# Gate one-hots of a retrieval layer: 24 narrow tensor_scalar instructions per step exchanged for two wide tensor_tensor instructions

## The chip, the cores and the metric

The kernel runs on one core of one Trainium2 chip. The time is device microseconds of one launch; three launches of the kernel before gave a median of 1547.26 us (1546.43 to 1547.27). Inside the core five engines work from queues of their own, in the order in which the program was written: TensorE (PE, with its weight loads as PEld), VectorE (DVE), ScalarE (ACT), GpSimd (POOL) and SyncE (SP). They wait for each other by semaphores.

## The reference

Two transformer-like blocks over 256 tokens of width 1024. The change lies in the second half of the first block, a retrieval over 128 x 128 single-neuron experts:

```python
s = einsum('thpk,hpnk->thpn', q, sub_keys)          # 8 heads, 2 key halves, 128 keys
sv, si = top_k(s, 16)                               # per half
cand = sv[..., 0, :, None] + sv[..., 1, None, :]    # 256 sums, the best 16 kept
fv, fpos = top_k(cand, 16)
eidx = take_along_axis(si0 * 128 + si1, fpos)       # 16 experts per token and head
g = softmax(fv)
act = gelu(einsum('td,thkd->thk', x, u_tab[eidx]))
y = einsum('thk,thkd->td', g * act, v_tab[eidx])
```

The kernel does not gather. It computes the activation of all 16384 experts for all tokens from the whole table `peer_u`, multiplies by a gate matrix that is zero for experts that were not chosen, and multiplies by the whole table `peer_v`.

## The kernel before, in words

Each of the 128 blocks of `peer_u` (128 experts, a weight tile of 128 x 1024) is one call of `U(b)`: 24 matmuls of 256 columns (L163 to L165, three products of split halves `whi`, `wlo`, `hi`, `lo` over eight pieces), then a GELU on ACT (L793). The halves of a weight tile are made ahead: ACT casts `whi` (L112, five tiles ahead), DVE subtracts `wlo` (L120, four tiles ahead).

The gate matrix is built for one token at a time. For token t there are 128 choices (8 heads x 16), one per partition: a row index, a column index and a gate value. With `o` the one-hot of the second index, and `go` the one-hot of the first index times the gate, the product of `o` and `go` over the partitions is the token's 128 x 128 gate matrix. The gate is kept as two 16-bit halves, so there are two `go` and two matmuls a token (L958). `onehots(og)` makes these tiles for eight tokens (OG = 8): per token one `tensor_scalar` for `o` (L941, compare the constant row 0..127 in `iob` with the index) and two for `go` (L943, compare and multiply), 24 in all. ACT then moves each bank of four tokens from PSUM to `stg`, scaled (L961), and every second step `stg` goes to DRAM as `gd` (L963).

The loop has 32 steps. In program order a step is: the one-hots of the next step, 16 gate matmuls in two groups of eight with an ACT move behind each, then one `U(b)`, which begins with the `whi` and `wlo` of later tiles. The `side` PSUM banks of the gate matmuls and the `main` banks of U are two each. Once the 32 steps are done, seven more U follow, and the loop over `peer_v` starts, which reads the gates back (`gt`). Nothing is scheduled by a planner: each engine's order is that of the code.

Of the kernel before, what the change touches and what calls it, by code (L numbers as in the profile page):

```python
# [13 lines left out]
F32 = mybir.dt.float32  # L14
F32R = mybir.dt.float32r
BF = mybir.dt.bfloat16
F16 = mybir.dt.float16
# [3 lines left out]
OP = mybir.AluOpType  # L21
# [4 lines left out]
T = 256  # L26
# [9 lines left out]
UKEEP = 7  # L36
TG = 16
OG = 8
GI = 8
LOADS = 9  # L40
SPLITS = 4
# [23 lines left out]
class Kx:  # L65
# [696 lines left out]
    def peer(self):  # L762
        nc, tc, a = self.nc, self.tc, self.a
# [4 lines left out]
        drp = ctx.enter_context(tc.tile_pool(name="pdr", bufs=1, space=DRAM))  # L768
        c1 = ExitStack()
        pz = c1.enter_context(tc.tile_pool(name="pz", bufs=1))  # L770
        gp = pz.tile([128, 2, T], F32, name="gp")
        ib = pz.tile([128, 2, T], F32, name="ib")
        acts = {}
        c2 = ExitStack()
        pk = c2.enter_context(tc.tile_pool(name="pk", bufs=1))
# [14 lines left out]
        def U(b):  # L790
            p = self.unit("peer_u", b, h)
            acts[b] = t = actp.tile([128, T], F32, name="act")
            nc.scalar.activation(t, p, AF.Gelu)  # L793

        pre = deque(range(2, NPRE))
        with c2:
# [39 lines left out]
            for hd in range(1, 8):  # L836
# [5 lines left out]
                for i in range(2 if hd > 1 else 0):  # L842
                    p = self.unit("w_query", 2 * hd + i, h)
# [11 lines left out]
            pf_ = c2.enter_context(tc.tile_pool(name="pf", bufs=1))  # L855
# [4 lines left out]
            def finish():  # L860
                g = [pf_.tile([128, 8, 16], F32, name=f"g{tt}") for tt in range(2)]
                pf = [pf_.tile([128, 2, 8, 16], F32, name=f"pf{tt}") for tt in range(2)]
                sxf = [pf_.tile([128, 2, 8, 16], F32, name=f"sxf{tt}") for tt in range(2)]
                for tt in range(2):
                    v = fv[tt]
                    nc.vector.tensor_tensor(g[tt], v, v[:, :, 0:1].to_broadcast([128, 8, 16]), op=OP.subtract)
                    nc.scalar.activation(g[tt], g[tt], AF.Exp)
                for tt in range(2):
                    pi = pft.tile([128, 2, 8, 16], U32, name="pi")
                    nc.vector.tensor_scalar(pi[:, 0], fx[tt], 4, None, op0=OP.logical_shift_right)  # L870
                    nc.vector.tensor_scalar(pi[:, 1], fx[tt], 15, None, op0=OP.bitwise_and)
                    nc.vector.tensor_copy(sxf[tt].rearrange("p s h a -> p h s a"), sx[tt])
                    nc.vector.tensor_copy(pf[tt], pi)
                for tt in range(2):
                    gz = pft.tile([128, 8], F32, name="gz")
                    nc.vector.tensor_reduce(gz, g[tt], axis=AX.X, op=OP.add)
                    nc.vector.reciprocal(gz, gz)
                    nc.vector.tensor_tensor(g[tt], g[tt], gz[:, :, None].to_broadcast([128, 8, 16]), op=OP.mult)
                for _ in range(FW):
                    yield  # L880
                for tt in range(2):
                    p = self.side()
                    for j, src in enumerate((sxf[tt][:, 0], sxf[tt][:, 1], pf[tt][:, 0], pf[tt][:, 1])):
                        nc.tensor.transpose(p[:, j * 128:(j + 1) * 128], src.rearrange("p a b -> p (a b)"),
                                            self.ident)
                    ts = slice(tt * 128, (tt + 1) * 128)
                    p = p.rearrange("p (k s t) -> p k s t", k=2, s=2)
                    nc.scalar.copy(sxT[:, :, ts], p[:, 0])
                    nc.scalar.copy(posT[:, :, ts], p[:, 1])
                p = self.side()  # L890
                for tt in range(2):
                    nc.tensor.transpose(p[:, tt * 128:(tt + 1) * 128], g[tt].rearrange("p a b -> p (a b)"),
                                        self.ident)
                slot = pf_.tile([128, T], F32, name="slot")
                nc.scalar.mul(slot, p[:, :T], GSCALE)
                yield
                acc = self.bank(0)
                last = None
                for a0 in range(0, 16, FA):
                    cur = []  # L900
                    for a in range(a0, a0 + FA):
                        pb = self.side()
                        nc.tensor.matmul(pb, pick[:, a].rearrange("p h w -> p (h w)"),
                                         sxT.rearrange("p s t -> p (s t)"), start=True, stop=True)
                        t = pft.tile([128, 2 * T], BF, name="hit", bufs=2 * FA)
                        nc.vector.scalar_tensor_tensor(t, posT.rearrange("p s t -> p (s t)"), float(a), pb,
                                                       op0=OP.is_equal, op1=OP.mult)
                        cur.append((a, t))
                    yield
                    for a, t in cur:  # L910
                        nc.tensor.matmul(acc, identb, t, start=a == 0, stop=a == 15)
                nc.scalar.copy(ib, acc.rearrange("p (j t) -> p j t", j=2))
                g16 = pf_.tile([128, T], F16, name="g16")
                nc.vector.tensor_copy(g16, slot)
                nc.vector.tensor_copy(gp[:, 0], g16)
                nc.vector.tensor_tensor(gp[:, 1], slot, gp[:, 0], op=OP.subtract)

            self.side_cycle = ("s", "s", "a1", "a2")
            self.tasks.append(finish())
            while self.tasks:  # L920
                self.tick()
                if len(pre) > T // OG + UKEEP:
                    U(pre.popleft())
            while len(pre) > T // OG + UKEEP:
                U(pre.popleft())
            self.side_cycle = ("s",)

        with ExitStack() as c3:
            pg = c3.enter_context(tc.tile_pool(name="pg", bufs=1))
            pgt = c3.enter_context(tc.tile_pool(name="pgt", bufs=2))  # L930
            iob = pg.tile([128, 128], F16, name="iob")
            nc.gpsimd.iota(iob, pattern=[[1, 128]], base=0, channel_multiplier=0,
                           allow_small_or_imprecise_dtypes=True)
            stg = None

            def onehots(og):
                o = pgt.tile([128, OG, 128], F16, name="o")
                go = pgt.tile([128, OG, 2, 128], F16, name="go")
                for i in range(OG):
                    t = slice(og * OG + i, og * OG + i + 1)  # L940
                    nc.vector.tensor_scalar(o[:, i], iob, ib[:, 1, t], None, op0=OP.is_equal)  # L941
                    for j in range(2):
                        nc.vector.tensor_scalar(go[:, i, j], iob, ib[:, 0, t], gp[:, j, t],  # L943
                                                op0=OP.is_equal, op1=OP.mult)
                return o, go

            nxt = onehots(0)
            for og in range(T // OG):
                o2, go = nxt
                if og + 1 < T // OG:  # L950
                    nxt = onehots(og + 1)
                if og % (TG // OG) == 0:
                    stg = pgt.tile([128, 128, TG], F32, name="stg")
                for q in range(OG // 4):
                    p = self.side().rearrange("p (t i) -> p t i", t=4)
                    for i in range(4):
                        for j in range(2):
                            nc.tensor.matmul(p[:, i], o2[:, q * 4 + i], go[:, q * 4 + i, j],  # L958
                                             start=i == 0 and j == 0, stop=j == 1, skip_group_check=True)
                    e0 = (og % (TG // OG)) * OG + q * 4  # L960
                    nc.scalar.mul(stg[:, :, e0:e0 + 4].rearrange("p i t -> p t i"), p, 1.0 / GSCALE)  # L961
                if og % (TG // OG) == TG // OG - 1:
                    nc.scalar.dma_start(gd[:, og * OG // TG], stg)  # L963
                if len(pre) > UKEEP:
                    U(pre.popleft())
# [3 lines left out]
        with ExitStack() as c4:  # L969
# [5 lines left out]
            def gload(i):  # L975
                if i * GI < NB:
                    gts[i] = gt = pv.tile([128, 8 * (T + 2)], F32, name="gt")[:, :8 * T].rearrange(
                        "p (g e) -> p g e", g=T // TG)
                    (nc.gpsimd if i < 2 else nc.scalar).dma_start(gt, gd[:, :, i * GI:(i + 1) * GI].rearrange("p g i t -> p g (i t)"))

            wts = {}

            def w_mult(b):
                if b >= NB:
                    return
                t = acts[b]
                gv = gts[b // GI][:, :, (b % GI) * TG:(b % GI + 1) * TG]
                tv = t.rearrange("p (g t) -> p g t", t=TG)
                nc.vector.tensor_tensor(tv, tv, gv, op=OP.mult)  # L989
                if b % GI == GI - 1:  # L990
                    gload(b // GI + 2)

# [583 lines left out]
```

## Time and profile before

| what | value |
|---|---|
| median of three launches | 1547.26 us |
| the profiled launch, own time | 1546.58 us |
| its span, first to last instruction | 1544.9 us |
| PE / PEld / DVE / ACT / POOL busy, share of the span | 92% / 87% / 78% / 50% / 16% |
| the 32 gate steps, first gate matmul to the last U's first matmul | 382.85 to 570.04 us |
| granted clock in that stretch | 0.94 |

Busy shares are averages over stages; a matmul's recorded duration overlaps the next one's, so that PE reads busy when it is well under its best rate. For PE the start-to-start distance of its instructions is the better measure, and the same holds for DVE and ACT where an instruction's record reaches over the start of the next.

### The profile page before, as it was taken

How to read it: one execution, taken by the hardware profiler on the slowest of the kernel's cores; microseconds unless marked ns; L12 is line 12 of the kernel's file. 1: busy time of each engine (PE TensorE's matmuls, PEld its weight loads, DVE VectorE, ACT ScalarE, POOL GpSimd, SP SyncE). 2: the span in 40 equal slices, each digit the busy share in tenths (PEclk: the TensorE clock that was granted, in tenths of full speed). 3: DMA queues.
4: the chain of work that ended last, by engine and by line, in shares of the span. 5: the costliest groups of instructions: out<-in, count | busy, mean ns of one | idle time of the engine just before them, and what ended most of it. 6: DMA issues, size and time to landing. Idle time of an engine off the chain costs nothing.

```text
span 1544.9 us, 28187 instructions
## 1 busy us (share of the span) xinstructions
PE 1427.4 (92%) x11206; PEld 1351.2 (87%) x11208; DVE 1204.3 (78%) x2723; ACT 765.9 (50%) x1225; POOL 240.9 (16%) x143
## 2 busy tenths in 40 slices
PE   3897888979998999999999999999989989999997
PEld 2777777978777779999999999999989979989997
DVE  7887789997999996777777776666689968775554
ACT  3445554434555555544444454454564485554443
POOL 1443253310000000000000000000057740310000
PEclk8898989989999999999999999999999999999999
DMA  9365543434444458888888887677534434435642
GB/s 377 141 239 181 191 150 136 154 122 162 161 167 186 169 206 308 297 307 312 303 308 286 294 285 233 219 244 241 179 114 163 164 109 164 164 138 190 205 165 81
DMA packets 106068, 317.36 MB, mean 205 GB/s; under 512 B 5584, under 2 KB 34640, under 8 KB 103632
## 3 DMA queue, kind: packets, MB, share of 16 engines
q1 hardware_dynamic: 65696, 250.54, 45.8%
q10 hardware_dynamic: 39408, 61.87, 11.4%
q0 software_dynamic: 832, 3.15, 0.6%
q8 instruction: 88, 1.44, 0.4%
q14 instruction: 44, 0.36, 0.1%
HBM read 297.71 MB, written 17.83 MB: 204 GB/s over the span
## 4 chain that ended last, share of the span: by engine, by line
PE 56%; DVE 34%; ACT 4%; DMA 3%; issue 2%; POOL 1%; DVEq 0%; SPq 0%; ACTq 0%; POOLq 0%
PE a L163 10%; PE a L164 10%; PE a L165 10%; PE m L163 8%; PE m L164 8%; PE m L165 8%; DVE go L943 7%; DVE wlo L120 5%; DVE a L1138 3%; DVE o L941 3%; DVE junk L326 2%; DMA mraw<-in_ada_w 1%; ACT whi L112 1%; DMA raw<-in_ada_w 1%; DVE mdt L294 1%
## 5 line engine op out<-in xcount | busy, mean ns | idle before, releaser
L163 PE MATMUL m<-hi,whi 128*128 128x256 f32 x1816 | 526.5, 290 | 9.2 <-DVE cacc L556 6.0
L165 PE MATMUL m<-hi,wlo 128*128 128x256 f32 x1816 | 516.9, 285 | 9.4 <-DVE wlo L120 9.4
L164 PE MATMUL m<-lo,whi 128*128 128x256 f32 x1816 | 517.0, 285 | 0.0
L112 ACT CAST whi<-raw 128x1024 fp32r<-128x1024 f32 x428 | 444.6, 1046 | 50.1 <-DMA raw<-in_peer_v 19.5
L120 DVE TENSOR_TENSOR wlo<-raw,whi 128x1024 fp32r<-128x1024 f32 x350 | 437.7, 1269 | 30.9 <-ACT whi L112 23.0
L163 PEld LDWEIGHTS m<-hi,whi 128*128 128x128 f32 x1816 | 352.1, 194 | 16.1 <-issue 5.4
L165 PEld LDWEIGHTS m<-hi,wlo 128*128 128x128 f32 x1816 | 351.1, 193 | 10.7 <-DVE wlo L120 10.4
L164 PEld LDWEIGHTS m<-lo,whi 128*128 128x128 f32 x1816 | 351.7, 194 | 0.6
L165 PE MATMUL a<-wh,wlo 128*128 128x256 f32 x1024 | 288.2, 281 | 0.0
L164 PE MATMUL a<-wl,whi 128*128 128x256 f32 x1024 | 288.2, 281 | 0.0
L163 PE MATMUL a<-wh,whi 128*128 128x256 f32 x1024 | 287.9, 281 | 0.0
L120 POOL TENSOR_TENSOR wlo<-raw,whi 128x1024 fp32r<-128x1024 f32 x81 | 202.2, 2510 | 223.0 <-ACT whi L112 196.1
L165 PEld LDWEIGHTS a<-wh,wlo 128*128 128x128 f32 x1024 | 192.9, 188 | 0.0
L164 PEld LDWEIGHTS a<-wl,whi 128*128 128x128 f32 x1024 | 192.7, 188 | 0.0
L163 PEld LDWEIGHTS a<-wh,whi 128*128 128x128 f32 x1024 | 192.7, 188 | 0.0
L1001 DVE TENSOR_TENSOR wl<-act,wh 128x256 fp32r<-128x256 f32 x128 | 54.5, 426 | 140.5 <-PE a L164 125.7
L793 ACT ACTIVATE act<-m 128x256 f32<-128x256 f32 x126 | 48.5, 385 | 197.6 <-PE m L165 197.4
L943 DVE TENSOR_SCALAR go<-iob,ib,gp 128x128 f16<-128x128 f16 x512 | 138.8, 319 | 0.0
L996 ACT CAST wh<-act 128x256 fp32r<-128x256 f32 x128 | 51.9, 406 | 141.7 <-DVE act L989 118.8
L326 DVE SCALAR_TENSOR_TENSOR junk<-mraw,silu 128x1024 bf16<-128x1024 f32 x80 | 104.2, 1303 | 6.3 <-DMA mraw<-in_ada_w 6.0
L220 POOL TENSOR_TENSOR act<-act 128x256 f32<-128x256 f32 x7 | 5.6, 800 | 548.7 <-ACT act L211 548.3
L958 PE MATMUL s<-go,o 128*128 128x128 f16 x512 | 74.1, 219 | 18.3 <-DVE go L943 17.5
(438 smaller groups left out, 1962.0 us busy)
## 6 DMA issues: line engine op xcount, KB each, us to landing
raw<-in_peer_u SPq DMA_DIRECT2D x64, 1024.0 KB, 5.8
raw<-in_peer_v SPq DMA_DIRECT2D x64, 1024.0 KB, 5.3
mraw<-in_w_ada ACTq DMA_DIRECT2D x48, 512.0 KB, 5.8
raw<-in_w_ffn_in SPq DMA_DIRECT2D x22, 1024.0 KB, 5.1
gd<-stg ACTq DMA_DIRECT2D x16, 1024.0 KB, 3.9
gt<-gd ACTq DMA_DIRECT2D x14, 1024.0 KB, 8.7
mraw<-in_ada_w SPq DMA_DIRECT2D x24, 512.0 KB, 3.8
raw<-in_w_ffn_out SPq DMA_DIRECT2D x11, 1024.0 KB, 5.0
```

Source lines behind the costliest of these rows:

```text
L112: self.nc.scalar.copy(t, self.raw[k])
L120: eng.tensor_tensor(t, self.raw.pop(k), h.bitcast(F32), op=OP.subtract)
L163: mm(out, w[0], x[0], start=start, stop=False, **kw)
L164: mm(out, w[0], x[1], start=False, stop=False, **kw)
L165: mm(out, w[1], x[0], start=False, stop=stop, **kw)
L326: self.nc.vector.scalar_tensor_tensor(junk, w, 0.5, self.silu_c[i], op0=OP.mult, op1=OP.mult, accum_out=self.mod[i][:, u:u + 1])
L793: nc.scalar.activation(t, p, AF.Gelu)
L941: nc.vector.tensor_scalar(o[:, i], iob, ib[:, 1, t], None, op0=OP.is_equal)
L943: nc.vector.tensor_scalar(go[:, i, j], iob, ib[:, 0, t], gp[:, j, t], op0=OP.is_equal, op1=OP.mult)
L958: nc.tensor.matmul(p[:, i], o2[:, q * 4 + i], go[:, q * 4 + i, j], start=i == 0 and j == 0, stop=j == 1, skip_group_check=True)
L996: nc.scalar.copy(wts[b], acts[b])
L1001: nc.vector.tensor_tensor(wl, acts.pop(b), wts[b].bitcast(F32), op=OP.subtract)
```

## The change

The indexes and both gate halves of all tokens are kept in one 16-bit tile `ig` instead of two float32 tiles. A new helper `spread(c)` has ACT write the values of 16 tokens out eight times each, side by side, into a tile `rep`. `onehots` then makes its tiles with two wide instructions over 2048 16-bit elements a partition: one `is_equal` gives the one-hots of both indexes, one `mult` multiplies the first of them by both gate halves. Repeated operands have a stride of zero on an outer dimension; the innermost run is eight elements long. The line numbers of the changed kernel are higher, by 2 ahead of this place and by 16 behind it.

```diff
+RC = 16
+RW = 8
...
-        gp = pz.tile([128, 2, T], F32, name="gp")
-        ib = pz.tile([128, 2, T], F32, name="ib")
+        ig = pz.tile([128, 2, T, 2], F16, name="ig")
+        ib, gp = ig[:, 0], ig[:, 1]
...
-                nc.scalar.copy(ib, acc.rearrange("p (j t) -> p j t", j=2))
-                g16 = pf_.tile([128, T], F16, name="g16")
-                nc.vector.tensor_copy(g16, slot)
-                nc.vector.tensor_copy(gp[:, 0], g16)
-                nc.vector.tensor_tensor(gp[:, 1], slot, gp[:, 0], op=OP.subtract)
+                nc.scalar.copy(ib.rearrange("p t j -> p j t"), acc.rearrange("p (j t) -> p j t", j=2))
+                nc.vector.tensor_copy(gp[:, :, 0], slot)
+                nc.vector.tensor_tensor(gp[:, :, 1], slot, gp[:, :, 0], op=OP.subtract)
...
+            rep = {}
+
+            def spread(c):
+                if c < T // RC:
+                    sh = [128, 2, RC * 2, RW]
+                    rep[c] = t = pgt.tile(sh, F16, name="rep")
+                    s = ig[:, :, c * RC:(c + 1) * RC].rearrange("p k t j -> p k (t j)")
+                    nc.scalar.copy(t, s[:, :, :, None].to_broadcast(sh))
+
             def onehots(og):
-                o = pgt.tile([128, OG, 128], F16, name="o")
+                c, r = divmod(og * OG, RC)
+                if r == 0:
+                    spread(c + 1)
+                sh = [128, 2 * OG, 128 // RW, RW]
+                i8, g8 = [rep[c][:, k, 2 * r:2 * (r + OG)][:, :, None, :].to_broadcast(sh) for k in range(2)]
+                o = pgt.tile([128, OG, 2, 128], F16, name="o")
                 go = pgt.tile([128, OG, 2, 128], F16, name="go")
-                for i in range(OG):
-                    t = slice(og * OG + i, og * OG + i + 1)
-                    nc.vector.tensor_scalar(o[:, i], iob, ib[:, 1, t], None, op0=OP.is_equal)
-                    for j in range(2):
-                        nc.vector.tensor_scalar(go[:, i, j], iob, ib[:, 0, t], gp[:, j, t],
-                                                op0=OP.is_equal, op1=OP.mult)
-                return o, go
+                v = lambda x: x.rearrange("p t j (a b) -> p (t j) a b", b=RW)
+                io = iob[:, None, :].to_broadcast([128, 2 * OG, 128]).rearrange("p t (a b) -> p t a b", b=RW)
+                nc.vector.tensor_tensor(v(o), i8, io, op=OP.is_equal)
+                nc.vector.tensor_tensor(go.rearrange("p t j (a b) -> p t j a b", b=RW),
+                                        o[:, :, 0:1].to_broadcast([128, OG, 2, 128]).rearrange("p t j (a b) -> p t j a b", b=RW),
+                                        g8.rearrange("p (t j) a b -> p t j a b", j=2), op=OP.mult)
+                return o[:, :, 1], go
+
+            spread(0)
```

On DVE, the order at the entry to the gate steps and through the first two sets of one-hots, of the kernel before (`wlo` is the subtraction for later U tiles):

```order
L120 TENSOR_TENSOR wlo<-raw,whi 128x1024 x6
L941 TENSOR_SCALAR o<-iob,ib 128x128
L943 TENSOR_SCALAR go<-iob,ib,gp 128x128 x2
...
L941 TENSOR_SCALAR o<-iob,ib 128x128
L943 TENSOR_SCALAR go<-iob,ib,gp 128x128 x2
L120 TENSOR_TENSOR wlo<-raw,whi 128x1024
```

The same place on DVE in the changed kernel:

```order
L122 TENSOR_TENSOR wlo<-raw,whi 128x1024 x6
L955 TENSOR_TENSOR o<-rep,iob 128x2048
L956 TENSOR_TENSOR go<-o,rep 128x2048
L955 TENSOR_TENSOR o<-rep,iob 128x2048
L956 TENSOR_TENSOR go<-o,rep 128x2048
L122 TENSOR_TENSOR wlo<-raw,whi 128x1024
```

The 24 narrow rows of a set have become two wide ones; the rows around them stand where they stood.

On ACT, the first three gate steps of the kernel before, from the GELU of the last U ahead of them:

```order
L793 ACTIVATE act<-m 128x256
L961 ACTIVATE stg<-s 128x4x128 x2
L112 CAST whi<-raw 128x1024
L793 ACTIVATE act<-m 128x256
L961 ACTIVATE stg<-s 128x4x128 x2
L963 DMA gd<-stg 128x2048
L112 CAST whi<-raw 128x1024
L793 ACTIVATE act<-m 128x256
L961 ACTIVATE stg<-s 128x4x128 x2
```

The same place on ACT in the changed kernel:

```order
L795 ACTIVATE act<-m 128x256
L943 COPY rep<-ig 128x512 x2
L977 ACTIVATE stg<-s 128x4x128 x2
L114 CAST whi<-raw 128x1024
L795 ACTIVATE act<-m 128x256
L943 COPY rep<-ig 128x512
L977 ACTIVATE stg<-s 128x4x128 x2
L979 DMA gd<-stg 128x2048
L114 CAST whi<-raw 128x1024
L795 ACTIVATE act<-m 128x256
L977 ACTIVATE stg<-s 128x4x128 x2
```

Two copies to `rep` stand behind the GELU of the U ahead of the first gate step, and one more in every second step, ahead of that step's moves to `stg`. The order on PE is unchanged.

## Rows read from the trace of the kernel before

**Rows 1.** The page: the chain that ended last, shares by line.

```profile
PE a L163 10%; PE a L164 10%; PE a L165 10%; PE m L163 8%; PE m L164 8%; PE m L165 8%; DVE go L943 7%; DVE wlo L120 5%; DVE a L1138 3%; DVE o L941 3%; DVE junk L326 2%; DMA mraw<-in_ada_w 1%; ACT whi L112 1%; DMA raw<-in_ada_w 1%; DVE mdt L294 1%
```

**Rows 2.** Busy time by stretch, inside and behind the gate steps.

```profile
core 0: us, PE busy (x) PEld busy (x) DVE busy (x) ACT busy (x) POOL busy (x), PEclk, DMA share, GB/s
...
480.00:490.00 10.00, 9.29 (x62) 8.05 (x62) 10.00 (x42) 5.49 (x6) 0.00 (x0) 0.83 0.51 185
...
580.00:590.00 10.00, 10.00 (x87) 10.00 (x86) 4.99 (x8) 4.83 (x9) 0.23 (x1) 1.00 1.02 331
```

**Rows 3.** Groups by line, 380 to 620 us: busy, mean ns, idle before, releaser.

```profile
L943 DVE TENSOR_SCALAR go<-iob,ib,gp 128x128 f16<-128x128 f16 x512 | 138.8, 319 | 0.0
...
L958 PE MATMUL s<-go,o 128*128 128x128 f16 x512 | 74.1, 219 | 18.3 <-DVE go L943 17.5
...
L941 DVE TENSOR_SCALAR o<-iob,ib 128x128 f16<-128x128 f16 x256 | 66.2, 259 | 0.0
```

**Rows 4.** DVE in time order: start us, duration us, instruction [idle before <-releaser].

```profile
473.30 0.54 DVE L943 TENSOR_SCALAR go<-iob,ib,gp 128x128 f16<-128x128 f16 x2
473.74 1.23 DVE L120 TENSOR_TENSOR wlo<-raw,whi 128x1024 fp32r<-128x1024 f32 x1
474.88 0.26 DVE L941 TENSOR_SCALAR o<-iob,ib 128x128 f16<-128x128 f16 x1
...
479.75 1.23 DVE L120 TENSOR_TENSOR wlo<-raw,whi 128x1024 fp32r<-128x1024 f32 x1
```

**Rows 5.** PE in time order, the same step.

```profile
471.85 0.43 PE L958 MATMUL s<-go,o 128*128 128x128 f16 x2 [0.17 <-DVE go L943]
...
473.92 0.36 PE L163 MATMUL m<-hi,whi 128*128 128x256 f32 x1
...
476.83 0.85 PE L958 MATMUL s<-go,o 128*128 128x128 f16 x8
```

**Rows 6.** PE, the first ten gate matmuls of the stage.

```profile
382.85 0.73 PE L958 MATMUL s<-go,o 128*128 128x128 f16 x10
```

**Rows 7.** ACT in time order: two moves to `stg` and what is behind them.

```profile
390.03 1.10 ACT L961 ACTIVATE stg<-s 128x512 f32<-128x512 f32 x1 [0.50 <-PE s L958]
...
391.60 1.05 ACT L112 CAST whi<-raw 128x1024 fp32r<-128x1024 f32 x1 [0.47 <-DVE go L943]
...
396.04 1.10 ACT L961 ACTIVATE stg<-s 128x512 f32<-128x512 f32 x1 [1.40 <-PE s L958]
396.92 1.08 ACT L112 CAST whi<-raw 128x1024 fp32r<-128x1024 f32 x1
```

**Rows 8.** ACT in time order, ahead of the gate steps.

```profile
342.98 1.04 ACT L112 CAST whi<-raw 128x1024 fp32r<-128x1024 f32 x1
343.92 0.39 ACT L793 ACTIVATE act<-m 128x256 f32<-128x256 f32 x1
344.19 0.38 ACT L888 CAST sxT<-a 128x256 bf16<-128x256 f32 x1
...
366.09 0.59 ACT L912 COPY ib<-a 128x512 f32<-128x512 f32 x1 [0.49 <-PE a L911]
366.57 1.05 ACT L112 CAST whi<-raw 128x1024 fp32r<-128x1024 f32 x1
...
383.05 0.39 ACT L793 ACTIVATE act<-m 128x256 f32<-128x256 f32 x1 [1.51 <-PE m L165]
```

**Rows 9.** DVE in time order, two of the preparing instructions.

```profile
365.27 0.28 DVE L914 CAST g<-slot 128x256 f16<-128x256 f32 x1
...
365.92 0.43 DVE L916 TENSOR_TENSOR gp<-slot,gp 128x256 f32<-128x256 f32 x1
```

**Rows 10.** PE, the first matmul of the last gate step's U.

```profile
570.04 0.37 PE L163 MATMUL m<-hi,whi 128*128 128x256 f32 x1
```

**Rows 11.** Busy time by stretch, a PE pause ahead of the stage.

```profile
334.00:336.00 2.00, 0.00 (x0) 0.00 (x0) 2.00 (x10) 0.00 (x0) 0.00 (x0) 1.00 0.00 0
336.00:338.00 2.00, 0.00 (x0) 0.00 (x0) 2.00 (x11) 0.00 (x0) 0.00 (x0) 0.59 0.00 0
```

## Prediction

> **What bounds the kernel now.** I read the chain of waits first: nearly all of it is PE, but 7% and 3% of the span are the narrow one-hot instructions L943 and L941 on DVE [rows 1]. So there is a stage in which DVE sets the pace. The table of busy time by stretch says where: inside the gate steps DVE is busy 10.00 of 10 us, PE less, and PE's granted clock falls to 0.83; behind them PE is at 10.00 with clock 1.00 and DVE at half [rows 2]. The groups by line show who waits: PE's gate matmuls stand idle for the releaser DVE L943, while both DVE groups have no idle time ahead of them [rows 3]. Recorded durations overlap, so I work with start-to-start distances.
>
> On DVE one step goes from one `wlo` to the next: 479.75 - 473.74 = 6.01 us. Of this `wlo` takes 474.88 - 473.74 = 1.14, and the 24 narrow instructions 4.87, or 0.203 each [rows 4]. On PE the gate matmuls come two at a time, each pair waiting for its token's one-hots; U itself runs from 473.92 to the next step's first gate matmul at 476.83, 2.91 us [rows 5]. What would the 16 gate matmuls take if nothing held them? The first ten of the stage, whose one-hots were ready, span 0.73 us; one of them lasts 0.219 [rows 3, 6], so they start (0.73 - 0.219) / 9 = 0.057 apart, and 16 take 0.91. With 0.03 for the turn to U, **PE needs 2.91 + 0.91 + 0.03 = 3.85 us a step and DVE makes it wait for 6.01.** That difference is what the change can win; behind the stage PE is full, so time won there is kept to the end.
>
> **The change, part by part.**
>
> *The wide instructions.* No row shows VectorE on two 16-bit tensors. The nearest row by operation is `wlo`, a float32 `tensor_tensor`: 1.23 us for 1024 elements against 0.43 for 256 [rows 4, 9], so 1.04 ns an element, which is 1.07 of its 1.14 us and leaves 0.07 fixed. At that rate 2048 elements take 2.13 + 0.07 = 2.20 us start to start. The nearest rows by element type are the casts to or from 16 bits: 256 elements in 0.28 us where `tensor_tensor` needs 0.43 [rows 9]. Taking the same 0.16 (0.43 less 256 at 1.04 ns) off both, the cast has 0.12 left for what costs 0.27 at one element a cycle, so it does two. At two, 2048 elements take 1.07 + 0.07 = 1.14, the same as `wlo`. The narrow rows don't decide: 128 elements at one a cycle plus 0.07 would be 0.20, which is their mean. I take two a cycle, because both sources and the result are 16-bit and run along consecutive addresses innermost, as in the casts; 2.20 stays as the other end.
>
> [...]
>
> The second wide instruction reads what the first wrote, so it starts behind the first's full duration (1.23) with some 0.05 for the semaphore. **DVE's new step: 1.23 + 0.05 + 1.14 + 1.14 (`wlo`) = 3.56 us**, under PE's 3.85. It stays under as long as the two wide instructions together cost no more than 2.71.
>
> *The copies to `rep` on ACT.* Each has 512 elements, one in two steps. The cheapest comparable row is the 512-element copy `ib`, 366.57 - 366.09 = 0.48 us start to start [rows 8]; the dearest is the strided move to `stg`, also 512, 396.92 - 396.04 = 0.88 [rows 7]. ACT's other work in two steps: GELU 344.19 - 343.92 = 0.27 and `whi` 343.92 - 342.98 = 0.94, twice each [rows 8]; four moves at 0.88; and the issue of the `gd` DMA, which makes one move cost 391.60 - 390.03 = 1.57 and so adds 0.69 [rows 7]. Sum 0.54 + 1.88 + 3.52 + 0.69 = 6.63, with a copy 7.11 to 7.51, against PE's 2 x 3.85 = 7.70. ACT stays just under; a copy above 1.07 us would make it the bound. In the loop each copy is made two steps ahead of its use, so its lateness costs DVE nothing.
>
> *The start.* Here the copies are not ahead. In program order both stand on ACT behind the GELU of the U in front of the gate steps. That GELU starts at 383.05 [rows 8], after PE reached the gate matmuls at 382.85 [rows 6]; before, DVE had made one-hots ahead of that. Now: copy from 383.05 + 0.27 = 383.32, done 0.6 later (the `ib` copy lasted 0.59) at about 383.95; first wide instruction to 385.2, second to 386.5. **PE stands still 3.65 us once**; with the dear copy 4.1. Such a pause can lower PE's clock: in the pause ahead of the stage the granted clock was 1.00 in the first two microseconds without a matmul and 0.59 in the next two [rows 11]. A dip like the one in the stage, 0.83 over 10 us [rows 2], is 3.4 us at half speed and gives away 1.7; I put 2 us, between 0 (none) and 5 (a dip three times as long).
>
> *Preparation.* One cast of 0.28 us goes, and the index copy now writes 16-bit elements two apart, at most 0.4 dearer by the ratio of the two ACT prices above. ACT waits 1.51 us ahead of its GELU there [rows 8], which covers it. Price nothing; 0.4 if the cover were gone.
>
> *Transfers.* The same bytes in shorter time: a DMA share of 0.51 and 185 GB/s become 0.51 x 6.01 / 3.85 = 0.80 and 289 GB/s; behind the stage the queues carry 331 GB/s with PE still at 10.00 [rows 2]. Price nothing.
>
> **The sum.** Before, PE goes from 382.85 [rows 6] to the last step's U at 570.04 [rows 10]: 187.2 us, which is 31 steps and one set of gate matmuls. After: 31 x 3.85 + 0.94 = 120.3, plus 3.65 for the start and 2 for the clock, 125.9. Saved: 61.3 us. The profiled launch took 1546.58 us, so 1485.3; it lies 0.7 under the median, so 1486 on the median's scale.
>
> **The rivals.**
>
> *One of the two wide instructions runs at one element a cycle.* DVE then has 1.23 + 0.05 + 2.20 + 1.14 = 4.62 a step and stays the bound: 31 x 4.62 + 0.94 + 4.7 (start) = 148.9, saved 38, so 1509. For it: two patterns of different depth, and no row of either. Against: both are of the same width and type.
>
> *Both run at one a cycle*, the change then saves only instruction starts: 2.29 + 0.05 + 2.20 + 1.14 = 5.68 a step, 31 x 5.68 + 0.94 + 5.8 = 182.8, saved 4.4, so 1543. For it: the only `tensor_tensor` rows there are show this rate. Against: they are all float32.
>
> *Slower than before: short runs cost a wide instruction extra.* ACT's move to `stg` takes 0.88 where a plain copy of the same 512 elements takes 0.48; it writes four consecutive words and hops. If VectorE paid the same 1.83 on its runs of eight, a wide instruction would take 1.83 x 2.13 + 0.07 = 3.97, a step 4.06 + 0.05 + 3.97 + 1.14 = 9.22, the stage 31 x 9.22 + 0.94 + 9.4 = 296, which is 109 more than now: 1656. The change loses from 4.87 us for the pair on, 2.43 each or 1.15 ns an element. Against it: the hops here are on inputs in SBUF, the outputs are consecutive.
>
> *PE's clock keeps dipping through the stage*, as it does now. PE would have no pauses to cause it, but if the lighter gate matmuls did, a dip each 24 us or so (five of them at 1.7) would cost 8.5 us: 1493. I hold it inside the forecast's range.
>
> **How the numbers follow.** Both at two a cycle: 0.82, with its own range from 1480 (no dip, cheap start) to 1497 (dips, dear copies). One at one a cycle 0.08, both 0.06, slower 0.04. The range 1479 to 1500 holds the first case and leaves out the other 0.18. A change of 0.2%, about 3 us, is what a measurement of this kernel can tell from none. The first two cases are faster; the third, at 4 us, is faster with half of its chance and the same with the other half. So faster 0.93, same 0.03, slower 0.04.
>
> **What would show it.** Right: L955 and L956 at about 1.23 us each, start-to-start of `wlo` 3.85 in the gate steps, PE idle there near nothing, DVE some 9.2 of 10 us, one PE wait of about 3.7 us for the first L956, and the gate steps some 126 us long. Wrong: either wide line at 2.3 us or more; copies to `rep` above 1.07 with PE waiting for ACT; or new waits for raw weight tiles, which would say that the transfers don't keep up at 3.85 us a step.

## The result and the profile after

The changed kernel takes 1484.53 us (median of four launches, 1482.17 to 1486.79) against 1547.15 before (four launches, one more than stood in the table): a ratio of 0.9596, 95% interval 0.9579 to 0.9613. The profiled launch took 1485.2 us, its span is 1483.5.

The page of the changed kernel, the same lines as [rows 1] with span and busy time ahead:

```profile
span 1483.5 us, 27484 instructions
...
PE 1379.9 (93%) x11206; PEld 1335.6 (90%) x11208; DVE 1124.5 (76%) x2018; ACT 765.6 (52%) x1241; POOL 242.6 (16%) x143
...
PE m L165 11%; PE m L166 11%; PE m L167 11%; PE a L167 10%; PE a L165 10%; PE a L166 10%; DVE wlo L122 3%; DVE a L1154 3%; PE s L974 2%; DVE junk L328 2%; DMA mraw<-in_ada_w 1%; DMA raw<-in_ada_w 1%; ACT whi L114 1%; DVE mdt L296 1%; DVE lo L303 1%
```

The one-hot lines, 10% of the chain before, are gone from it; in their place stands 2% of PE's own gate matmuls (L974). Busy time by stretch, inside and behind the gate steps, as in [rows 2]:

```profile
440.00:450.00 10.00, 10.00 (x110) 9.86 (x110) 9.00 (x9) 8.95 (x13) 0.00 (x0) 1.00 0.83 276
...
480.00:490.00 10.00, 10.00 (x104) 9.91 (x102) 9.46 (x9) 9.34 (x13) 0.00 (x0) 1.00 0.84 305
...
520.00:530.00 10.00, 10.00 (x87) 10.00 (x86) 6.78 (x10) 5.37 (x10) 0.00 (x0) 1.00 1.01 349
```

PE is full at clock 1.00, with over 100 matmuls in 10 us where it had 62; DVE and ACT have become the ones that are nearly full. Groups by line in the gate steps, as in [rows 3]:

```profile
L956 DVE TENSOR_TENSOR go<-o,rep 128x2048 f16<-128x2048 f16 x32 | 39.2, 1225 | 1.1
L955 DVE TENSOR_TENSOR o<-rep,iob 128x2048 f16<-128x2048 f16 x32 | 39.0, 1219 | 4.1 <-ACT rep L943 4.1
L974 PE MATMUL s<-go,o 128*128 128x128 f16 x512 | 34.1, 220 | 3.6 <-DVE go L956 3.6
...
L943 ACT COPY rep<-ig 128x512 f16<-128x512 f16 x16 | 9.7, 610 | 0.0
```

Both wide instructions take 1.22 us, DVE's one-hots 78 us instead of 205, and all of PE's wait for them is one of 3.6 us. DVE in time order, as in [rows 4], then PE, as in [rows 5], then ACT over two steps:

```profile
434.22 1.23 DVE L122 TENSOR_TENSOR wlo<-raw,whi 128x1024 fp32r<-128x1024 f32 x1 [0.42 <-ACT whi L114]
435.36 1.22 DVE L955 TENSOR_TENSOR o<-rep,iob 128x2048 f16<-128x2048 f16 x1
436.62 1.23 DVE L956 TENSOR_TENSOR go<-o,rep 128x2048 f16<-128x2048 f16 x1
437.76 1.22 DVE L122 TENSOR_TENSOR wlo<-raw,whi 128x1024 fp32r<-128x1024 f32 x1
```

```profile
498.03 1.07 PE L974 MATMUL s<-go,o 128*128 128x128 f16 x16
498.90 0.36 PE L165 MATMUL m<-hi,whi 128*128 128x256 f32 x1
...
501.82 1.07 PE L974 MATMUL s<-go,o 128*128 128x128 f16 x16
```

```profile
430.22 0.61 ACT L943 COPY rep<-ig 128x512 f16<-128x512 f16 x1
430.73 2.01 ACT L977 ACTIVATE stg<-s 128x512 f32<-128x512 f32 x2
...
437.53 0.39 ACT L795 ACTIVATE act<-m 128x256 f32<-128x256 f32 x1 [0.29 <-PE m L167]
437.81 0.61 ACT L943 COPY rep<-ig 128x512 f16<-128x512 f16 x1
```

A step is 501.82 - 498.03 = 3.79 us on PE; DVE needs 437.76 - 434.22 = 3.54 of it. ACT repeats every 437.81 - 430.22 = 7.59 us, two steps, and waits 0.29 of them for PE. The start of the stage, all engines:

```profile
383.26 1.13 ACT L943 COPY rep<-ig 128x512 f16<-128x512 f16 x2
383.97 1.23 DVE L955 TENSOR_TENSOR o<-rep,iob 128x2048 f16<-128x2048 f16 x1 [4.06 <-ACT rep L943]
385.23 1.23 DVE L956 TENSOR_TENSOR go<-o,rep 128x2048 f16<-128x2048 f16 x1
...
386.51 1.05 PE L974 MATMUL s<-go,o 128*128 128x128 f16 x16 [3.56 <-DVE go L956]
...
391.81 1.07 PE L974 MATMUL s<-go,o 128*128 128x128 f16 x16
```

DVE stands idle for the copies, PE for DVE; the first step then takes 391.81 - 386.51 = 5.30 us, because part of it runs at a lower granted clock, 0.68 and 0.64 in the two stretches of 4 us that hold it, and the matmuls of its U start 0.21 us apart from 388.06 to 390.62 where it is 0.12 in the step from 498.90:

```profile
386.00:390.00 4.00, 3.49 (x29) 3.49 (x29) 3.97 (x5) 2.85 (x3) 0.00 (x0) 0.68 0.00 0
388.00:392.00 4.00, 4.00 (x27) 3.96 (x26) 3.97 (x4) 2.00 (x3) 0.00 (x0) 0.64 0.00 0
```

### The profile page after: what moved, and what is told of

Its sections match the earlier page's. It is cut to its first block, busy times and chain, and to the rows that moved or that the text cites. A ratio compares the mean times of both kernels' runs of the same rounds, so it can differ in the third digit from the quotient of the medians.

```text
span 1483.5 us, 27484 instructions
## 1 busy us (share of the span) xinstructions
PE 1379.9 (93%) x11206; PEld 1335.6 (90%) x11208; DVE 1124.5 (76%) x2018; ACT 765.6 (52%) x1241; POOL 242.6 (16%) x143
## 4 chain that ended last, share of the span: by engine, by line
PE 68%; DVE 23%; ACT 4%; DMA 3%; issue 2%; POOL 1%; DVEq 0%; SPq 0%; ACTq 0%; POOLq 0%
PE m L165 11%; PE m L166 11%; PE m L167 11%; PE a L167 10%; PE a L165 10%; PE a L166 10%; DVE wlo L122 3%; DVE a L1154 3%; PE s L974 2%; DVE junk L328 2%; DMA mraw<-in_ada_w 1%; DMA raw<-in_ada_w 1%; ACT whi L114 1%; DVE mdt L296 1%; DVE lo L303 1%
## 5 line engine op out<-in xcount | busy, mean ns | idle before, releaser
L977 ACT ACTIVATE stg<-s 128x512 f32<-128x512 f32 x64 | 64.7, 1120 | 3.0 <-PE s L974 2.8
L1005 DVE TENSOR_TENSOR act<-act,gt 128x256 f32<-128x256 f32 x128 | 53.6, 419 | 4.5 <-DMA gt<-gd 4.5
```

## The experiments

**What sets the rate of the wide instructions.** Four kernels change only what they read. First, no copies: both read index or gate as one element repeated innermost.

```diff
-                nc.vector.tensor_tensor(v(o), i8, io, op=OP.is_equal)
+                ts = slice(og * OG, (og + 1) * OG)
+                i1, g1 = [ig[:, k, ts].rearrange("p t j -> p (t j)")[:, :, None].to_broadcast([128, 2 * OG, 128])
+                          for k in range(2)]
+                nc.vector.tensor_tensor(o.rearrange("p t j n -> p (t j) n"), i1,
+                                        iob[:, None, :].to_broadcast([128, 2 * OG, 128]), op=OP.is_equal)
...
-                                        g8.rearrange("p (t j) a b -> p t j a b", j=2), op=OP.mult)
+                                        g1.rearrange("p (t j) n -> p t j n", j=2), op=OP.mult)
```

> The copies to rep are gone; both wide instructions read the index or gate as one element repeated innermost. If the rate hangs on innermost runs (my theory): about 2.3 us each, DVE step 2.3+0.05+2.2+1.14 = 5.7, no start wait for copies, stage 31 x 5.7 + 3 = 179, so about 1538. If 16-bit width alone gives the rate (rival): 1.22 each, PE stays the bound at 3.79 a step and the start wait shrinks, so about 1481.

Second, only the `is_equal` is changed so.

> Only the is_equal reads single repeated elements; the mult still reads rep. My theory: 2.3 and 1.22 us, DVE step 2.3+0.05+1.14+1.14 = 4.63, DVE is the bound again, stage 31 x 4.63 + 5.6 = 149, so about 1508. Rival (width alone): both 1.22, step 3.79, 1485.

Third, two copies of each value (`RW = 2`) instead of eight.

> Values written out twice instead of eight times: innermost runs of two elements, one 4-byte word. If a run of two is enough for two results a cycle: wide instructions 1.22 each, step 3.79, copies to rep shorter (about 0.3), so 1484 to 1486. If short runs cost extra cycles at each hop: between 1.6 and 2.2 us each, DVE step 4.3 to 5.6, 1500 to 1540.

Fourth, those two copies kept in float32.

```diff
-RW = 8
+RW = 2
...
-                    rep[c] = t = pgt.tile(sh, F16, name="rep")
+                    rep[c] = t = pgt.tile(sh, F32, name="rep")
```

> rep holds float32 values, twice each, instead of 16-bit ones; the row, the result and o stay 16-bit. If all tensors must be 16 bits wide (my theory): both wide instructions 2.3 us, step about 5.7 as with single elements, start wait about 5.4: 1545. If consecutive runs alone gave the rate: 1.22 each, 1486.

Groups by line of the first kernel:

```profile
L953 DVE TENSOR_TENSOR go<-o,ig 128x2048 f16<-128x2048 f16 x32 | 73.3, 2292 | 1.1
...
L951 DVE TENSOR_TENSOR o<-ig,iob 128x2048 f16<-128x2048 f16 x32 | 73.1, 2284 | 0.0
...
L968 PE MATMUL s<-go,o 128*128 128x128 f16 x496 | 33.1, 220 | 52.4 <-DVE go L953 52.4
```

and of the second:

```profile
L958 DVE TENSOR_TENSOR o<-ig,iob 128x2048 f16<-128x2048 f16 x32 | 73.1, 2285 | 0.0
...
L960 DVE TENSOR_TENSOR go<-o,rep 128x2048 f16<-128x2048 f16 x32 | 39.2, 1226 | 2.9 <-ACT rep L943 1.8
```

Single elements: 2.28 us each and 1544.76 us in all (1538 expected; 1546.74 for the kernel before beside it), PE waiting for DVE. One of the two: 2.285 and 1.226, 1511.43 (1508 expected). Both also lost time behind the gate steps, 6.4 and 5.3 us, which no expectation had; a table further down takes that up. Two copies: the two lines stay at 1.218 and 1.225 us and the time at 1487.12, with a copy of 0.289 us (128 elements) instead of 0.609 (512).

```profile
L955 DVE TENSOR_TENSOR o<-rep,iob 128x2048 f16<-128x2048 f16 x32 | 39.0, 1218 | 3.7 <-ACT rep L943 3.7
```

Float32 copies (a row names the type of the first input alone; in the second it is `o`):

```profile
383.35 2.29 DVE L955 TENSOR_TENSOR o<-rep,iob 128x2048 f16<-128x2048 f32 x1 [3.74 <-ACT rep L943]
385.68 2.29 DVE L956 TENSOR_TENSOR go<-o,rep 128x2048 f16<-128x2048 f16 x1
```

2.29 us each, 1545.23. So in these kernels 16-bit width alone does not give the rate (2.28 us with single elements), and consecutive runs alone do not (2.29 with float32 copies); with both, runs of two are enough (1.22). The difference, 2.285 - 1.222 = 1.063 us, is what 1024 elements take at the 1.04 ns an element of `wlo` in the kernel before: by this estimate, beside a fixed part, the one rate is twice the other.

**Is ACT the next bound?** The copies to `rep` are made two or three times over.

```diff
-                    nc.scalar.copy(t, s[:, :, :, None].to_broadcast(sh))
+                    for _ in range(3):
+                        nc.scalar.copy(t, s[:, :, :, None].to_broadcast(sh))
```

> Each copy to rep is made three times. ACT has now about 7.16 us of work in two steps against PE's 7.58; two more copies at 0.51 to 0.6 make 8.2 to 8.4, so ACT becomes the bound at 4.1 to 4.2 a step, and the start waits 1 us or so longer: 1485 + 31 x 0.35 + 1 = 1497. If ACT is not close to its limit, only the start shows: 1486.

> Each copy to rep is made twice. ACT then has 7.16 + 0.6 = 7.76 in two steps, just over PE's 7.58: step 3.8 to 3.9, and the start waits 0.6 longer: 1486 to 1490. If ACT had ample room: 1486.

Three: 1501.71, two: 1494.03, both over what was expected. ACT in time order with two copies, two steps apart, and with three; then PE's waits in the gate steps with three:

```profile
439.38 1.28 ACT L944 COPY rep<-ig 128x512 f16<-128x512 f16 x2
440.57 1.99 ACT L978 ACTIVATE stg<-s 128x512 f32<-128x512 f32 x2
...
447.22 1.29 ACT L944 COPY rep<-ig 128x512 f16<-128x512 f16 x2
```

```profile
440.49 2.02 ACT L978 ACTIVATE stg<-s 128x512 f32<-128x512 f32 x2
...
448.95 2.01 ACT L978 ACTIVATE stg<-s 128x512 f32<-128x512 f32 x2
```

```profile
PE s L975 <- ACT stg L978: 7.4, 26, 0.3
PE s L975 <- DVE go L957: 4.9, 1, 4.9
```

With two, 7.84 us for two steps; with three, 8.46, and PE waits 26 times for ACT. From the first to the last gate matmul it is 122.7 and 131.0 us instead of 120.0. ACT is the next bound, just behind PE, as expected. But that is 2.7 and 11.0 us, while the spans grew by 8.8 and 16.5. The first gate matmul starts at 386.5 and 387.2 (386.5 in the changed kernel), so most of the rest is lost behind the last one: from there to the second block's first copy of `v1` it is 574.9 and 573.1 us instead of 566.9, so 8.0 and 6.2 more. The second block then gives 1.9 and 1.4 back. PE's wait behind the gate steps, with two copies:

```profile
PE m L165 <- ACT act L795: 5.0, 1, 5.0
```

With three it is 3.5 us. The changed kernel has no such wait. What the pause costs beyond itself comes with the next kernels.

**Less work on PE, and where the gain goes.** The second gate half is left out of the matmuls: eight gate matmuls a step instead of sixteen.

```diff
-                        for j in range(2):
-                            nc.tensor.matmul(p[:, i], o2[:, q * 4 + i], go[:, q * 4 + i, j],
-                                             start=i == 0 and j == 0, stop=j == 1, skip_group_check=True)
+                        nc.tensor.matmul(p[:, i], o2[:, q * 4 + i], go[:, q * 4 + i, 0],
+                                         start=i == 0, stop=True, skip_group_check=True)
```

> The second gate half is left out of the matmuls (8 gate matmuls a step instead of 16), everything else stays. PE's step falls from 3.79 to about 3.34. If ACT is next (7.16 in two steps = 3.58, DVE 3.56): step 3.6, gain 31 x 0.19 = 6, about 1479. If PE alone counted: 31 x 0.45 = 14, about 1471.

The gate steps fell from 120.0 to 113.4 us, a step of about 3.6, just as if ACT came next; yet the time was 1486.27. In this kernel, first the PE wait behind the steps, then DVE and ACT at that place:

```profile
PE m L165 <- ACT act L795: 5.9, 1, 5.9
```

```profile
524.90 0.43 DVE L1004 TENSOR_TENSOR act<-act,gt 128x256 f32<-128x256 f32 x1 [12.44 <-DMA gt<-gd]
```

```profile
525.40 0.41 ACT L1011 CAST wh<-act 128x256 fp32r<-128x256 f32 x1 [9.48 <-DVE act L1004]
525.71 1.04 ACT L114 CAST whi<-raw 128x1024 fp32r<-128x1024 f32 x1
526.66 0.38 ACT L795 ACTIVATE act<-m 128x256 f32<-128x256 f32 x1
```

Read from the top: PE wants a `main` bank that the GELU has to empty; the GELU stands on ACT behind `wh`, `wh` waits for DVE's product with the gates, and that for the gates to come back from DRAM. To test this reading, nine U instead of seven were kept for behind the steps (`UKEEP = 9`), with the half gates still left out.

> The second gate half is left out of the matmuls again, and nine U calls instead of seven stand behind the gate steps, two fewer ahead of them. If the 5.9 us that PE lost behind the steps were the way of the gates through DRAM: the wait goes (two U are 5.6 us more cover), 1486.3 - 5.9 = 1480. If it had another cause: 1486.

1478.45 (1480 expected), and the wait fell from 5.9 to 0.4 us. The way of the gates through DRAM is what took the gain away again. How long that way is, from the last gate matmul to DVE's first product with the gates, can be read from every kernel's trace, with PE's wait beside it (the early start is described further down):

| kernel | way of the gates, us | PE's wait, us | last gate matmul to `v1`, us |
|---|---|---|---|
| before | 15.7 | none | 567.0 |
| changed, two profiles | 15.9, 17.6 | none | 566.9, 567.0 |
| two copies of each value; early start; both | 16.1; 17.1; 15.8 | none | 567.0 each |
| single elements | 21.4 | 3.6 | 573.4 |
| one of the two | 21.4 | 3.6 | 572.3 |
| float32 copies | 21.5 | 3.6 | 572.4 |
| copies made three times | 21.4 | 3.5 | 573.1 |
| copies made twice | 22.8 | 5.0 | 574.9 |
| half gates | 23.8 | 5.9 | 575.5 |
| half gates, nine U | 23.9 | 0.4 | 573.3, two U more in it |

With seven U the way less the wait is 17.8 or 17.9 us wherever PE waits: that much of the way PE's own work covers. Two more U, at 2.83 us each, make 23.5, and 23.9 less 0.4 is just that. It is the way that got longer, not the cover that got shorter: with half gates the last gate matmul comes 5.4 us earlier than in the changed kernel, but the gates are back 2.5 us later (524.9 against 522.4), and the three kernels with slow wide instructions wait too, although their gate steps are longer. What makes the way 16 us in one kernel and over 21 in another was not tried.

The pause costs more than itself. With half gates 8.6 us are lost up to `v1` for a wait of 5.9, and PE's granted clock reads 0.56 and 0.58 in the two stretches of 4 us in which PE starts again and goes on (525 to 533), where it stays at 1.00 with nine U (520 to 528).

**The start.** Two U are held back and placed behind the first copies and one-hots.

```diff
+EARLY = 2
...
-            while len(pre) > T // OG + UKEEP:
+            while len(pre) > T // OG + UKEEP + EARLY:
...
             nxt = onehots(0)
+            for _ in range(EARLY):
+                U(pre.popleft())
```

> Two U calls are held back and stand behind the first copies and the first one-hots, so that both are made while PE works. My theory: the PE wait of 3.56 us at the first gate matmul and the clock dip behind it (1.7 us) go, the step stays 3.79: 1484.5 - 5.3 = 1479. Rival: the wait is not on the path because the two weight tiles prepared later then hold PE up instead: 1484.

> The changed kernel once more, on the chip of the other runs of this call: 1482 to 1487, and the place of its clock dips behind the stage to vary from launch to launch by about 2 us.

> As the early start, with the values written out twice instead of eight times. The wide instructions stay at 1.22 us and ACT has 0.3 us less per two steps; PE is the bound, so no further gain: 1479, the same as the early start within 2 us.

> The early start with nine U calls behind the gate steps. With the early start PE had no wait behind the steps in its profile, so no gain in the fast launches: 1478, as with seven. If some launches lose time there, the median falls by 1 to 3 us and the spread narrows.

Start of the stage in the early kernel:

```profile
380.31 1.23 DVE L956 TENSOR_TENSOR o<-rep,iob 128x2048 f16<-128x2048 f16 x1 [4.07 <-ACT rep L944]
381.57 1.22 DVE L957 TENSOR_TENSOR go<-o,rep 128x2048 f16<-128x2048 f16 x1
...
384.78 1.07 PE L977 MATMUL s<-go,o 128*128 128x128 f16 x16
```

```profile
380.00:390.00 10.00, 10.00 (x102) 9.91 (x102) 9.58 (x9) 7.49 (x12) 0.00 (x0) 1.00 0.37 127
```

The one-hots are ready 2 us ahead and PE has no wait; the clock stays at 1.00. Against the kernel before, on one chip: early 1477.98 us, ratio 0.9546 (0.9534 to 0.9558); the changed kernel 1485.61, 0.9594 (0.9582 to 0.9607); early with two copies 1479.67, 0.9557 (0.9535 to 0.9579), with launches from 1472.25 to 1485.11. The early start wins 7.6 us where 5.3 was expected, and beats both kernels. Shorter copies add nothing that these launches could show, PE being the bound. With nine U kept, on another chip: 1479.98, 0.9558 (0.9545 to 0.9571), no gain either, since the profile of the early kernel has no wait there. For the changed kernel's repetition, clock dips that move from launch to launch by some 2 us were expected behind the stage; its one further profile shows no such difference, its second block taking 410.0 us where it was 410.1.

## Why the prediction was right

**The rate of the wide instructions.** Taken as 1.14 us start to start and 1.23 in duration; measured 437.76 - 436.62 = 1.14 and 1.22. No row of before showed it: the 1.14 was the author's estimate from the casts, and one element "a cycle" stands there for the 1.04 ns an element of `wlo`, since no run shows VectorE's clock. What the rate hangs on was seen in the four kernels: a wide instruction that reads single elements, or one float32 input, takes 2.28 to 2.29 us, one whose tensors are all 16-bit and read in runs of two takes 1.22. The rivals at the slower rate came out near their forecasts, 1511.43 for 1509 and 1544.76 (or 1545.23) for 1543, but with 5.3 to 6.4 us lost behind the steps that the forecasts did not have. With both wide instructions at the slower rate the change comes out at about a tie: 1544.76 against 1546.74 and 1545.23 against 1545.9 in single launches.

**DVE's new step** of 3.56 measured 3.54, under PE's, as forecast. **PE's step** of 3.85 measured 3.79: 16 gate matmuls and the turn to U take 498.90 - 498.03 = 0.87, not 0.94, fifteen distances of 0.057 and next to nothing for the turn. Over 31 steps that is 1.9 us more gain.

**ACT.** Forecast 7.11 to 7.51 in two steps; it works or waits on its own work 7.59 - 0.29 = 7.30. The copy was near the cheap end, 430.73 - 430.22 = 0.51. The forecast that a copy above 1.07 us would make ACT the bound held: copying twice costs 440.57 - 439.38 = 1.19, and two steps take 7.84.

**The start.** 3.65 forecast, 3.56 measured, through the very chain that was written down; the clock 2 forecast, 5.30 - 3.79 = 1.5 measured. The early start removes both, which shows that they were on the path.

**The sum.** From PE's arrival at the gate matmuls (386.51 - 3.56 = 382.95) to the last step's (506.5) it is 123.5 us against 187.1 before (382.9 to 570.0): 63.6 saved, 61.3 forecast. The profiled launch saved 1546.58 - 1485.2 = 61.4, so 2.2 were lost behind it, which the prediction did not have. They are lost in the second block: from the first copy of `v1` to the end it is 407.9 us before (1137.0 to 1544.9) and 410.1 after (1073.4 to 1483.5). The code there is the same. In the early kernel the same stretch took 407.7, in the second profile of the changed kernel 410.0. By matched instructions the changed kernel is 63.5 us ahead at 1165.2 (on the time scale of the kernel before), 62.8 at 1239.1 and 61.7 at 1245.7, so most of the loss falls into or between two stretches whose granted clock differs, before and after:

```profile
1157.00:1177.00 20.00, 18.16 (x138) 17.69 (x137) 18.14 (x38) 8.95 (x15) 15.24 (x8) 0.91 0.51 180
...
1237.00:1257.00 20.00, 16.89 (x114) 15.00 (x115) 14.63 (x40) 17.00 (x45) 10.34 (x5) 0.91 0.42 135
```

```profile
1093.40:1113.40 20.00, 16.74 (x117) 16.19 (x116) 17.27 (x36) 8.51 (x15) 14.83 (x7) 0.83 0.53 163
...
1173.40:1193.40 20.00, 16.71 (x108) 15.26 (x108) 14.31 (x37) 15.82 (x44) 10.14 (x4) 0.83 0.36 117
```

In the stretch of 20 us ahead of the first pair it is the other way round, 0.91 before and 1.00 after. So the lower clock falls on other work, which fits the 2 us; that it is the cause, and what decides where it falls, was not tried. The closeness of 1484.5 to 1486 is in part luck: two errors of 2 us cancel. The early start's 7.6 us instead of 5.3 split in the same way: of the 7.1 between the two launches profiled (1486.72 and 1479.62), 4.8 are there at the last gate matmul (508.0 and 503.2) and 2.3 come in the second block (410.0 and 407.7).

**What the prediction passed over.** "Time won there is kept to the end" is true for the changed kernel, but only just. The prediction put no number to the cover that seven U give behind the steps, and it priced the transfers at nothing. By the table the cover is 17.8 us, and the gates need 15.9 us in one profile of the changed kernel and 17.6 in the other, where it was 15.7 before. DVE waits 4.5 and 6.2 us for them (4.3 before), ACT 1.6 in the first, PE not at all. In six of the experiments the way is over 21 us, and 5.3 to 8.6 us go behind the steps. That the changed kernel stayed within its cover is luck as far as the prediction goes: it weighed the load of the queues there, not the time that the gates need.

## What to carry to other kernels

Many narrow instructions with per-partition scalars can be exchanged for one wide one with two tensor operands. Here that won with every tensor 16 bits wide and an innermost run of two or eight consecutive elements (1.22 us for 2048 elements), and came to about a tie with single elements or float32 copies in both wide instructions (2.28 to 2.29 us); a copy of 0.29 or 0.61 us on ACT, which had room for it, provides that run. Before counting on the gain, work out the step of each other engine, since the new time is that of the next one (here 3.79 on PE, with ACT and DVE within 7% of it), and look at both ends of the stage: what must exist before its first step, and whether the work behind it covers the way of its result.

## What was not expected of the hardware

Writing a value out twice is as good as eight times: 1.22 us either way for 2048 elements. And the same 1 MB writes of `gd`, with the same shape, land a median of 7.1 us after their issue where it was 3.9 before, while the mean DMA share of the gate steps went from 0.46 to 0.74. Before and after:

```profile
gd<-stg ACTq DMA_DIRECT2D x16, 1024.0 KB, 3.9
```

```profile
gd<-stg ACTq DMA_DIRECT2D x16, 1024.0 KB, 7.1
```

The other kernels lie in the order of their steps: 3.9 us with a wide instruction at the slow rate, 5.4 with the copies made three times, 6.5 with two, 8.2 with half gates. That the denser transfers make the longer landing was not tried by itself.
